# One operation per column for product and difference in a 32-step forward substitution

## The chip, the core and the metric

The kernel runs on one core of a Trainium2 chip. A core has a matrix engine (TensorE, PE in the rows; its weight loads are PEld), three engines for elementwise work (VectorE, DVE; ScalarE, ACT; GpSimd, POOL) and a queue that issues most transfers (SP). Each engine works through its own queue in order, and engines wait for each other by semaphores. The metric is the time of the program on the device in microseconds, median of the runs.

## What is computed

A decoder block on 256 tokens of width 2048: a SwiGLU block, a token mixer (8 gated DeltaNet heads beside 16 Mamba-2 heads), a second SwiGLU block and gated embeddings. The change is in the DeltaNet heads, in the inverse of a unit lower triangular matrix for each head and each chunk of tokens:

```python
lower = jnp.where(strict, jnp.einsum('bnhik,bnhjk->bnhij', kb, k) * decay, 0.0)
eye = jnp.eye(CHUNK, dtype=q.dtype)
t_inv = lax.linalg.triangular_solve(eye + lower, jnp.broadcast_to(eye, lower.shape),
                                    left_side=True, lower=True)
u = jnp.einsum('bnhij,bnhjv->bnhiv', t_inv, v * beta[..., None])
w = jnp.einsum('bnhij,bnhjk->bnhik', t_inv, kb * jnp.exp(gc)[..., None])
```

## The kernel before

All large products are float32 products made of pieces: a weight tile is loaded (`load`), each 128 x 1024 piece of it is rounded on ACT (`hi`, L118), the rest is taken on DVE (`lo`, L119), and PE multiplies both (`single`, L145 to L147: 8 blocks of three matmuls in a piece). There are four buffers each for `hi` and `lo`, so ACT and DVE can be four pieces ahead of PE and no more.

The mixer's input projection is 50 tiles of two such pieces, one after another, with the convolutions (L557), gates and scalings of each tile on DVE. The work of the heads is written as generators; `tick()` after each piece advances every open generator by one step, and the scheduler then puts the instructions of each engine in an order by dependences and a timeline of its own. So the work of the heads stands between pieces, in the queues of the same engines.

`gdn_pair(i, KQ, V)` does a pair of heads, and there are four pairs. A pair has four 128 x 128 matrices. It computes the lower triangles (`LA`, L601 to L609), writes their 32 x 32 diagonal blocks to memory (`blkl`, four transfers on POOL's queue, L630) and reads them back with the blocks spread over partitions (`Lb`, SP's queue, L632). Each of 128 partitions then holds one 32 x 32 block and four columns `Z[:, c, :]` of its inverse (`CG = 4`, `BS = 32`). `Z` starts as unit columns (L656). The substitution has 31 steps, three to a tick: step `j` multiplies the rest of column `j` of the block by `Z[:, c, j]` for all four columns at once into `tb` (L663), and takes it from the rest of `Z` (L665). A row `128x124` in the profile is four columns of 31, `128x4` four of 1. Then `Z` goes to memory (`blky`, L666), comes back in blocks (`Y`, four transfers, L671), is transposed (L674) and is merged in two levels by matmuls on PE (`ip`, `ix`, `iy`, L685) with masks and differences on DVE (L700, L690) between them; then follow the outputs of the two chunks (L714 to L758). `Lb`, `Z` and `tb` have one buffer each: the substitution of a pair begins when the one before has been stored.

Of the kernel before, what the change touches and what calls it, by code (L numbers as in the profile page):

```python
# [9 lines left out]
F32 = mybir.dt.float32  # L10
F32R = mybir.dt.float32r
AF = mybir.ActivationFunctionType
ALU = mybir.AluOpType
PSUM = bass.MemoryType.PSUM

P = 128
# [27 lines left out]
BS = 32  # L44
CG = 4
# [23 lines left out]
def tile_hybrid_block(ctx, tc, xT, pT, con, par, wgu1, wd1, wnar, win, wout, wgu2, wd2, wproj, wple, outT):  # L69
    nc = tc.nc  # L70
    act, dve, pool, pe = nc.scalar, nc.vector, nc.gpsimd, nc.tensor
# [25 lines left out]
    def over(ap, n):  # L97
        return ap.unsqueeze(1).to_broadcast([ap.shape[0], n, ap.shape[-1]])
# [263 lines left out]
    with ExitStack() as mix:  # L362
# [213 lines left out]
        def gdn_pair(i, KQ, V):  # L576
# [16 lines left out]
            for c in range(2):  # L593
# [5 lines left out]
                for hh in range(2):  # L599
                    m = 2 * c + hh  # L600
                    dve.scalar_tensor_tensor(out=LA[:, m, 0, :], in0=ps[:, hh * T:hh * T + P], scalar=1.0, in1=ident,  # L601
                                             op0=ALU.mult, op1=ALU.mult, accum_out=ss[:, m:m + 1])
# [4 lines left out]
                              in1=beta[:, :, h0:h0 + 2], op=ALU.mult)  # L607
            for m, (c, hh) in enumerate(mats):
                dve.scalar_tensor_tensor(  # L609
                    out=LA[:, m, :, :], in0=kk[c][:, hh * T:(hh + 1) * T].rearrange("p (a i) -> p a i", a=2),  # L610
                    scalar=c1[:, m:m + 1], in1=over(d[:, c, hh, :], 2), op0=ALU.mult, op1=ALU.mult)
# [19 lines left out]
            Lb = g2.tile([P, BS, BS], F32, tag="Lb", name="Lb", bufs=1)  # L631
            nc.sync.dma_start(Lb.rearrange("p j i -> p (j i)"),  # L632
                              bl.rearrange("q j i -> q (j i)").unsqueeze(1).to_broadcast([P // NG, NG, BS * BS]))
            Z = g2.tile([P, CG, BS], F32, tag="Z", name="Z", bufs=1)
            tb = g2.tile([P, CG * BS], F32, tag="tb", name="tb", bufs=1)

            Y = g2.tile([P, 4, P], F32, tag="Y", name="Y")
            pool.memset(Y, 0.0)
# [19 lines left out]
            for j in range(BS - 1):  # L658
                if j % STEP == 0:
                    yield  # L660
                n = BS - 1 - j
                t = tb[:, :CG * n].rearrange("p (c n) -> p c n", n=n)
                dve.tensor_tensor(out=t, in0=over(Lb[:, j, j + 1:], CG),  # L663
                                   in1=Z[:, :, j:j + 1].to_broadcast([P, CG, n]), op=ALU.mult)
                dve.tensor_tensor(out=Z[:, :, j + 1:], in0=Z[:, :, j + 1:], in1=t, op=ALU.subtract)  # L665
            nc.gpsimd.dma_start(by.rearrange("q c i -> (q c i)").rearrange("(p f) -> p f", p=P),  # L666
                              Z.rearrange("p c i -> p (c i)"))

# [62 lines left out]
            for hh in range(2):  # L731
                dve.scalar_tensor_tensor(out=y1[:, hh, :], in0=pk[:, hh, :], scalar=negc[:, h0 + hh:h0 + hh + 1],
                                         in1=y1[:, hh, :], op0=ALU.mult, op1=ALU.add)
# [28 lines left out]
        g2 = gdn_pool.enter_context(tc.tile_pool(name="g2", bufs=2))  # L762
# [4 lines left out]
        def delta_rule(i):  # L767
            KQ = g2.tile([P, 2, 2, T], F32, tag="KQ", name="KQ", bufs=3)
            V = g2.tile([P, 2, T], F32, tag="V", name="V", bufs=1)
            for which in range(3):  # L770
                j = 6 * i + 2 * which
                conv_silu(j, gcw[:, j:j + 2, :], None, V if which == 2 else KQ[:, :, which, :])
            drain([scalars_done])
            gdn.append(begin(gdn_pair(i, KQ, V)))
# [97 lines left out]
        for g in range(2):  # L872
            sacc = new_acc()
            for i in (2 * g, 2 * g + 1):
# [3 lines left out]
                                         op0=ALU.mult, op1=ALU.mult)  # L878
# [17 lines left out]
        op = mix.enter_context(tc.tile_pool(name="op", bufs=1))  # L896
# [48 lines left out]
    with tc.tile_pool(name="f2", bufs=2) as f2:  # L945
# [31 lines left out]
        for o in range(0, KD, 2):  # L977
            last = o == KD - 2
            t = f2.tile([P, 2, T], F32, tag="t", name="t")
            for j, n in ((0, 1), (1, 1)) if last else ((0, 2),):  # L980
# [4 lines left out]
                else:  # L985
                    for i in range(j, j + n):
# [5 lines left out]
                                         op0=ALU.add, op1=ALU.mult)  # L992
# [105 lines left out]
```

## Time and profile before

| | |
|---|---|
| median of 3 runs | 2078.45 us (2074.31 to 2078.91) |
| the profiled execution, own time | 2073.93 us |
| its span, first to last instruction | 2072.0 us |
| PE busy | 2049.0 us (99%) |
| DVE busy | 1362.2 us (66%) |
| ACT busy | 1035.1 us (50%) |
| POOL busy | 175.6 us (8%) |
| first product of the substitution to last difference | 838.0 to 1058.9 us |

Busy is the time in which an engine has at least one instruction under way. A span of 2072.0 us cut into 40 slices gives 51.8 us each, and the digits of the page are tenths of busy time in a slice. Times of rows are microseconds from the start of the span.

### The profile page before, as it was taken

The page shows a single profiled execution, that of the slowest core. Times are in us where ns is not written, and L with a number is a line of the kernel's source. Part 1 is how long each engine was busy: PE and PEld are TensorE (multiplying, and loading weights), DVE is VectorE, ACT ScalarE, POOL GpSimd, SP SyncE. Part 2 cuts the span into 40 slices and gives each one's busy share as a digit, 9 for nine tenths or more (in the row PEclk, how much of TensorE's full clock was granted, in tenths as well). Part 3 has the DMA queues.
Part 4 walks back from the last instruction along what each step waited for, and adds up shares of the span by engine and source line. Part 5 has one row for each costly group of instructions (what it writes and reads, how often), then busy time and mean ns, then how long its engine had stood idle before and what let it go on. Part 6 is the DMA issues. An engine that isn't in the chain of part 4 may idle for free.

```text
span 2072.0 us, 31523 instructions
## 1 busy us (share of the span) xinstructions
PE 2049.0 (99%) x12882; PEld 1832.2 (88%) x12882; DVE 1362.2 (66%) x2063; ACT 1035.1 (50%) x1544; POOL 175.6 (8%) x207
## 2 busy tenths in 40 slices
PE   9999999999999999999999999999999999999997
PEld 7888888888888889999999998888888888888886
DVE  7565555555656668999887666555555565556675
ACT  6444444444444555645545456444444444445554
POOL 2000000000000013413321111000000000000011
PEclk9999999999999999999999999999999999999998
DMA  7555555655555666554545555555556555545652
GB/s 266 190 186 183 171 176 194 211 183 183 186 184 178 197 219 218 184 179 164 162 166 173 190 179 189 190 183 184 167 184 217 182 184 185 191 162 190 208 183 102
DMA packets 64369, 384.58 MB, mean 186 GB/s; under 512 B 7616, under 2 KB 9168, under 8 KB 31072
## 3 DMA queue, kind: packets, MB, share of 16 engines
q1 hardware_dynamic: 61456, 376.75, 52.6%
q0 software_dynamic: 2480, 5.29, 0.8%
q8 instruction: 101, 1.65, 0.3%
q10 hardware_dynamic: 288, 0.52, 0.1%
q14 instruction: 44, 0.36, 0.0%
HBM read 377.78 MB, written 4.75 MB: 185 GB/s over the span
## 4 chain that ended last, share of the span: by engine, by line
PE 92%; DVE 3%; DMA 2%; issue 2%; POOL 1%; ACT 1%; POOLq 0%; DVEq 0%; SPq 0%; ACTq 0%
PE mm L130 50%; PE mm L128 24%; PE mm L146 4%; PE mm L147 4%; PE mm L145 4%; PE mm L132 1%; DVE lo L119 1%; DMA hT<-rows 1%; PE pj L130 0%; PE ip L685 0%; DMA blkl<-LA 0%; DMA blky<-Z 0%; DVE u L557 0%; PE iy L685 0%; POOL hT L820 0%
## 5 line engine op out<-in xcount | busy, mean ns | idle before, releaser
L119 DVE TENSOR_TENSOR lo<-raw,hi 128x1024 fp32r<-128x1024 f32 (+1 forms) x774 | 862.5, 1122 | 482.2 <-ACT hi L118 481.4
L130 PE MATMUL mm<-xs,hi 128*128 128x512 f32 x3088 | 1078.4, 397 | 0.7 <-DVE xs L190 0.7
L118 ACT CAST hi<-raw 128x1024 fp32r<-128x1024 f32 (+1 forms) x774 | 744.3, 963 | 558.8 <-PE mm L130 369.3
L128 PE MATMUL mm<-xs,lo 128*128 128x256 f32 x2895 | 812.7, 281 | 2.0 <-DVE lo L119 2.0
L130 PEld LDWEIGHTS mm<-xs,hi 128*128 128x128 f32 x3088 | 568.0, 188 | 124.6 <-DVE xs L190 1.2
L128 PEld LDWEIGHTS mm<-xs,lo 128*128 128x128 f32 x2895 | 543.5, 188 | 13.3 <-DVE lo L119 3.2
L130 PE MATMUL mm<-hid,hi 128*128 128x512 f32 x1408 | 492.5, 397 | 0.0
L128 PE MATMUL mm<-hid,lo 128*128 128x256 f32 x1344 | 377.8, 281 | 0.0
L130 PEld LDWEIGHTS mm<-hid,hi 128*128 128x128 f32 x1408 | 260.2, 188 | 59.0
L128 PEld LDWEIGHTS mm<-hid,lo 128*128 128x128 f32 x1344 | 253.3, 188 | 3.0
L147 PE MATMUL mm<-xs,lo 128*128 128x256 f32 x816 | 229.4, 281 | 3.4 <-DVE lo L119 3.4
L145 PE MATMUL mm<-xs,hi 128*128 128x256 f32 x816 | 229.7, 282 | 0.0
L146 PE MATMUL mm<-xs,hi 128*128 128x256 f32 x816 | 229.0, 281 | 0.0
L147 PEld LDWEIGHTS mm<-xs,lo 128*128 128x128 f32 x816 | 154.3, 189 | 4.1 <-DVE lo L119 4.0
L146 PEld LDWEIGHTS mm<-xs,hi 128*128 128x128 f32 x816 | 154.4, 189 | 0.4
L145 PEld LDWEIGHTS mm<-xs,hi 128*128 128x128 f32 x816 | 154.2, 189 | 0.6 <-issue 0.3
L168 ACT COPY t<-mm 128x256 f32<-128x256 f32 x167 | 62.2, 373 | 161.7 <-PE mm L130 160.6
L205 POOL TENSOR_TENSOR acc<-acc,sq 128x512 f32<-128x512 f32 x43 | 62.3, 1449 | 945.3 <-ACT sq L204 906.8
L169 DVE TENSOR_TENSOR t<-t,mm 128x256 f32<-128x256 f32 x167 | 69.9, 419 | 87.8 <-ACT t L168 87.5
L168 ACT COPY s<-mm 128x256 f32<-128x256 f32 x88 | 32.8, 372 | 149.0 <-PE mm L130 148.9
L169 DVE TENSOR_TENSOR s<-s,mm 128x256 f32<-128x256 f32 x88 | 37.1, 421 | 74.0 <-ACT s L168 73.9
L147 PE MATMUL mm<-osp,lo 128*128 128x256 f32 x256 | 71.8, 281 | 0.0
(304 smaller groups left out, 1444.1 us busy)
## 6 DMA issues: line engine op xcount, KB each, us to landing
raw<-in_wgu SPq DMA_DIRECT2D x173, 1024.0 KB, 4.8
raw<-in_wd SPq DMA_DIRECT2D x128, 704.0 KB, 4.1
raw<-in_win SPq DMA_DIRECT2D x52, 1024.0 KB, 4.8
raw<-in_wout SPq DMA_DIRECT2D x16, 1024.0 KB, 4.8
raw<-in_wple SPq DMA_DIRECT2D x16, 1024.0 KB, 4.8
first<-in_wgu SPq DMA_DIRECT2D x11, 256.0 KB, 7.2
hold<-hT POOLq DMA_DIRECT2D x4, 512.0 KB, 3.9
Lb<-blkl SPq DMA_DIRECT2D x4, 512.0 KB, 4.6
```

Of the source, the lines that this page charges most:

```text
L118: act.copy(hi, src)
L119: dve.tensor_tensor(out=lo, in0=src, in1=hi.bitcast(F32), op=ALU.subtract)
L128: pe.matmul(ps[:, 0, :], lo[:, w, :], act_in[:, k, 0, :], start=False, stop=False, skip_group_check=True)
L130: pe.matmul(ps, hi[:, w, :], act_in[:, k], start=start, stop=stop, skip_group_check=True)
L132: pe.matmul(ps[:, 0, :], lo[:, w, :], act_in[:, k, 0, :], start=False, stop=False, skip_group_check=True)
L145: pe.matmul(ps[:, 0, :], hi[:, i, :], act_in[:, k, 0, :], start=k == ks[0], stop=False)
L146: pe.matmul(ps[:, 0, :], hi[:, i, :], act_in[:, k, 1, :], start=False, stop=False)
L147: pe.matmul(ps[:, 0, :], lo[:, i, :], act_in[:, k, 0, :], start=False, stop=k == ks[-1])
L168: act.copy(out, ps[:, 0, :])
L169: dve.tensor_tensor(out=out, in0=out, in1=ps[:, 1, :], op=ALU.add)
L205: pool.tensor_tensor(out=acc, in0=acc, in1=sq, op=ALU.add)
```

## The change

The product and the difference of a step become one operation for each of the four columns, `Lb * z - Z` instead of `Z - Lb * z`. The sign of what remains turns at every step, so the odd entries of a column come out negated, and one multiplication by -1 on ACT turns them back before `Z` is stored. `tb` goes.

```diff
             Z = g2.tile([P, CG, BS], F32, tag="Z", name="Z", bufs=1)
-            tb = g2.tile([P, CG * BS], F32, tag="tb", name="tb", bufs=1)
...
             for j in range(BS - 1):
                 if j % STEP == 0:
                     yield
-                n = BS - 1 - j
-                t = tb[:, :CG * n].rearrange("p (c n) -> p c n", n=n)
-                dve.tensor_tensor(out=t, in0=over(Lb[:, j, j + 1:], CG),
-                                   in1=Z[:, :, j:j + 1].to_broadcast([P, CG, n]), op=ALU.mult)
-                dve.tensor_tensor(out=Z[:, :, j + 1:], in0=Z[:, :, j + 1:], in1=t, op=ALU.subtract)
+
+                for c in range(CG):
+                    dve.scalar_tensor_tensor(out=Z[:, c, j + 1:], in0=Lb[:, j, j + 1:], scalar=Z[:, c, j:j + 1],
+                                             in1=Z[:, c, j + 1:], op0=ALU.mult, op1=ALU.subtract)
+            odd = Z.rearrange("p c (i s) -> p c i s", s=2)[:, :, :, 1]
+            act.mul(odd, odd, -1.0)
             nc.gpsimd.dma_start(by.rearrange("q c i -> (q c i)").rearrange("(p f) -> p f", p=P),
                               Z.rearrange("p c i -> p (c i)"))
```

For a pair that is 124 operations in place of 62 on DVE, and one more on ACT. In the changed file the copy of unit columns is L655, the new operation L662, the negation L665 and the other lines named here up to one lower or the same.

The scheduler gives the engines another order. The first of three places is DVE's queue where the third pair begins. Before, two pieces `lo` of the projection stand between the last difference of the second pair (L665) and the copy that starts the third pair's `Z` (L656).

```order
L665 TENSOR_TENSOR Z<-Z,tb 128x4
L557 SCALAR_TENSOR_TENSOR u<-cin,gcw,u 128x256 x2
L119 TENSOR_TENSOR lo<-raw,hi 128x1024
L557 SCALAR_TENSOR_TENSOR u<-cin,gcw,u 128x256
L382 TENSOR_TENSOR cin<-mm,r 128x256
L119 TENSOR_TENSOR lo<-raw,hi 128x1024
L557 SCALAR_TENSOR_TENSOR u<-cin,gcw,u 128x256 x2
L656 COPY Z<-cont 128x128
```

The same place of the changed kernel, from the last step of the second pair (L662 `128x1`).

```order
L662 SCALAR_TENSOR_TENSOR Z<-Lb,Z 128x1 x4
L557 SCALAR_TENSOR_TENSOR u<-cin,gcw,u 128x256 x6
L382 TENSOR_TENSOR cin<-mm,r 128x256 x2
L655 COPY Z<-cont 128x128
L561 SCALAR_TENSOR_TENSOR V<-th,u 128x512
L662 SCALAR_TENSOR_TENSOR Z<-Lb,Z 128x31 x4
L662 SCALAR_TENSOR_TENSOR Z<-Lb,Z 128x30
L119 TENSOR_TENSOR lo<-raw,hi 128x1024
```

No piece stands between them any more. On ACT the negation of the second pair (L665) stands behind the scaling of the first pair's outputs (L753), which waits for a chain of small operations on POOL.

```order
L753 ACTIVATE o<-o,ro 128x128 x4
L552 ACTIVATE u<-cin,gcw 128x256 x2
L586 ACTIVATE ksq<-KQ 128x512
L665 ACTIVATE Z<-Z 128x64
```

The second place is DVE's queue where the fourth pair begins. Before: the last product and difference of the third pair (L663, L665 `128x4`) with a piece between them, two more pieces, the copy, a fourth piece.

```order
L663 TENSOR_TENSOR tb<-Lb,Z 128x4
L119 TENSOR_TENSOR lo<-raw,hi 128x1024
L557 SCALAR_TENSOR_TENSOR u<-cin,scw,u 128x256
L665 TENSOR_TENSOR Z<-Z,tb 128x4
L557 SCALAR_TENSOR_TENSOR u<-cin,scw,u 128x256
L814 TENSOR_TENSOR xd<-xt,sp 128x256 x2
L119 TENSOR_TENSOR lo<-raw,hi 128x1024
L557 SCALAR_TENSOR_TENSOR u<-cin,scw,u 128x256
L817 TENSOR_TENSOR xe<-xd,dte 128x256
L119 TENSOR_TENSOR lo<-raw,hi 128x1024
L656 COPY Z<-cont 128x128
L119 TENSOR_TENSOR lo<-raw,hi 128x1024
```

The same place of the changed kernel, from the last step of the third pair (L662 `128x1`) on, with the fourth pair's `LA` (L609) and the third pair's transpose (L674).

```order
L662 SCALAR_TENSOR_TENSOR Z<-Lb,Z 128x1
L609 SCALAR_TENSOR_TENSOR LA<-kk,c_9675,hT 128x256 x4
L614 TENSOR_TENSOR kdw<-c_9675,dte 128x2
L119 TENSOR_TENSOR lo<-raw,hi 128x1024
L814 TENSOR_TENSOR xd<-xt,sp 128x256 x2
L655 COPY Z<-cont 128x128
L817 TENSOR_TENSOR xe<-xd,dte 128x256
L662 SCALAR_TENSOR_TENSOR Z<-Lb,Z 128x31 x4
L662 SCALAR_TENSOR_TENSOR Z<-Lb,Z 128x30 x4
L674 STREAM_TRANSPOSE oT<-Y 128x512
L662 SCALAR_TENSOR_TENSOR Z<-Lb,Z 128x29 x4
```

One piece instead of two stands between the last step and the copy, `LA` of the fourth pair has moved to the place right behind that step, and the transpose stands behind the first eight new operations. No further `lo` follows until 69 of the fourth pair's 124 operations have been issued.

The third place is PE's queue at the merge of the third pair. Before, a piece of the projection (L145 to L147) stands between `iy` of the first level and `ip` of the second.

```order
L685 MATMUL iy_9843<-Y,blockQ 128x64 x4
L811 MATMUL xt<-cont,XS 128x128 x4
L145 MATMUL mm<-xs,hi 128x256
L146 MATMUL mm<-xs,hi 128x256
L147 MATMUL mm<-xs,lo 128x256
...
L685 MATMUL ip_9902<-oT,LA 128x64 x4
```

The same in the changed kernel.

```order
L758 MATMUL ot<-cont,o 128x128 x4
L685 MATMUL ip_9918<-oT,LA 128x64
L824 MATMUL ss_9924<-xe,Bt 128x256
L685 MATMUL ip_9918<-oT,LA 128x64 x3
L832 MATMUL py<-hT,xd 64x128 x8
L836 MATMUL yo<-BC,St 128x128 x2
L685 MATMUL ix_10023<-blockQ,Y 128x64 x4
L685 MATMUL iy_10028<-Y,blockQ 128x64 x4
L811 MATMUL xt<-cont,XS 128x128 x4
L685 MATMUL ip_10093<-oT,LA 128x64 x4
L145 MATMUL mm<-xs,hi 128x256
```

Here the first level, both differences and `ip` of the second level stand in one block without a piece of the projection between them. The merges of the second, third and fourth pair begin after 60, 74 and 86 of the 100 pieces before, and after 64, 76 and 87 now; the first after 44 before and 49 now.

## Rows read from the trace of the kernel before

**Rows 1.** Page, busy tenths in 40 slices.

```profile
PE   9999999999999999999999999999999999999997
DVE  7565555555656668999887666555555565556675
```

**Rows 2.** Busy time by stretch: PE, PEld, DVE, ACT, POOL, clock, DMA share, GB/s.

```profile
837.90:1058.90 221.00, 214.86 (x1853) 210.95 (x1852) 204.17 (x547) 117.33 (x215) 57.28 (x83) 0.99 0.51 176
880.00:900.00 20.00, 17.94 (x142) 17.73 (x142) 19.79 (x44) 8.46 (x12) 4.70 (x5) 0.91 0.46 163
1060.00:1160.00 100.00, 100.00 (x866) 99.71 (x865) 70.51 (x101) 52.79 (x84) 18.84 (x27) 1.00 0.50 173
```

**Rows 3.** Groups of DVE by line, 830 to 1062 us: busy, mean ns | idle before.

```profile
L665 DVE TENSOR_TENSOR Z<-Z,tb 128x124 f32<-128x124 f32 (+30 forms) x124 | 30.4, 245 | 1.3
L663 DVE TENSOR_TENSOR tb<-Lb,Z 128x124 f32<-128x124 f32 (+30 forms) x124 | 30.3, 245 | 4.9 <-DMA Lb<-blkl 3.5
```

**Rows 4.** DVE in order of time: start, duration in us, instruction [idle before].

```profile
935.23 0.21 DVE L663 TENSOR_TENSOR tb<-Lb,Z 128x48 f32<-128x48 f32 x1
935.47 0.21 DVE L665 TENSOR_TENSOR Z<-Z,tb 128x48 f32<-128x48 f32 x1
...
936.45 0.34 DVE L732 SCALAR_TENSOR_TENSOR xv<-ks,negc,xv 128x128 f32<-128x128 f32 x1
936.71 0.68 DVE L561 SCALAR_TENSOR_TENSOR KQ<-th,u 128x512 f32<-128x512 f32 x1
...
939.00 0.48 DVE L557 SCALAR_TENSOR_TENSOR u<-cin,gcw,u 128x256 f32<-128x256 f32 x1
939.39 0.19 DVE L663 TENSOR_TENSOR tb<-Lb,Z 128x36 f32<-128x36 f32 x1
939.51 0.48 DVE L557 SCALAR_TENSOR_TENSOR u<-cin,gcw,u 128x256 f32<-128x256 f32 x1
```

**Rows 5.** Waits of DVE, then of PE, 837.9 to 1058.9: total us, times, longest.

```profile
DVE Z L656 <- DMA blky<-Z: 5.1, 3, 3.0
DVE tb L663 <- DMA Lb<-blkl: 3.5, 1, 3.5
DVE lo L119 <- ACT hi L118: 2.3, 3, 1.1
...
PE ip L685 <- DVE oT L674: 3.0, 2, 1.6
PE mm L147 <- DVE lo L119: 2.3, 2, 2.1
```

**Rows 6.** DVE in order of time where the fourth pair begins.

```profile
1000.89 1.26 DVE L609 SCALAR_TENSOR_TENSOR LA<-kk,c,hT 128x256 f32<-128x256 f32 x3
...
1003.74 0.16 DVE L665 TENSOR_TENSOR Z<-Z,tb 128x4 f32<-128x4 f32 x1
...
1012.02 0.23 DVE L656 COPY Z<-cont 128x128 f32<-128x128 f32 x1 [3.05 <-DMA blky<-Z]
...
1016.87 0.29 DVE L663 TENSOR_TENSOR tb<-Lb,Z 128x124 f32<-128x124 f32 x1 [3.49 <-DMA Lb<-blkl]
...
1020.01 0.71 DVE L674 STREAM_TRANSPOSE oT<-Y 128x512 f32<-128x512 f32 x1
```

**Rows 7.** POOL in order of time at the same place.

```profile
1006.54 0.59 POOL L666 DMA_DIRECT2D blky<-Z  x1
...
1012.28 2.21 POOL L671 DMA_DIRECT2D Y<-blky  x4 [1.83 <-DMA blky<-Z]
```

**Rows 8.** PE in order of time, within one piece.

```profile
1014.73 0.28 PE L145 MATMUL mm<-xs,hi 128*128 128x256 f32 x1
...
1016.43 0.28 PE L145 MATMUL mm<-xs,hi 128*128 128x256 f32 x1
```

**Rows 9.** DVE in order of time after the last difference of the fourth pair.

```profile
1058.77 0.16 DVE L665 TENSOR_TENSOR Z<-Z,tb 128x4 f32<-128x4 f32 x1
...
1067.28 0.70 DVE L674 STREAM_TRANSPOSE oT<-Y 128x512 f32<-128x512 f32 x1
```

## The prediction

> **What bounds the kernel now.** I read the page first. PE is busy in every slice, and DVE, at 66% over the span, reaches nine tenths in slices 17 to 19, which lie in the mixer [rows 1]. The table by stretch says more: from the first product of the substitution to the last difference, 221.0 us, DVE is busy for 204.2 and PE for 214.9; from 1060 to 1160 us DVE needs 70.5 of 100 and PE all of it [rows 2]. So PE sets the time of the whole, but in the stretch that the change touches DVE has 221.0 - 204.2 = 16.8 us left and little else to give. The waits say how PE stays fed: it waits for `lo` for 2.3 us in the stretch, and for the transpose before a merge for 3.0 [rows 5]. Of DVE's own 16.8 us, 5.1 are waits of the copy that starts `Z` for the store of the pair before, and 3.5 a wait for `Lb` [rows 5]: the chain of the pairs, not spare time.
>
> **The price of one new operation.** DVE starts an instruction that waits for nothing before the one ahead has ended, so I count from start to start. An operation of this kind with a scalar per partition takes 936.71 - 936.45 = 0.26 us for 128 columns and 939.39 - 939.00 = 0.39 for 256 [rows 4], that is 1.02 ns a column and 0.13 us fixed. The new ones have 31 to 1 columns, 16 on average: 0.13 + 0.016 = 0.146 us. There are 4 pairs x 31 x 4 = 496: 72.4 us. No row shows one so small. A bound from below is the small product, 939.51 - 939.39 = 0.12 us for 36 columns [rows 4], 0.10 for 16; a bound from above is the duration at 128 columns less 112 columns, 0.34 - 0.114 = 0.226 us, which it would take if each waited for the one ahead. It need not: it reads what the operation four places before it wrote, and 4 x 0.146 = 0.58 us is longer than 0.226. I take 0.146 because its kind and scalar are those of the two rows it comes from.
>
> [...]
>
> **What they replace.** The 248 old ones, L663 and L665, last 30.3 + 30.4 = 60.7 us [rows 3]. A product overlaps its neighbour by 0.07 us where that does not wait (0.19 long, next start after 0.12), and where the difference follows directly, the gap is 0.24 for 0.21 [rows 4]. Added from start to start, without idle time, they take 48.3. So DVE gets 72.4 - 48.3 = +24 us; with 0.13 to 0.16 us for one, +16 to +31.
>
> **What covers it.** Of the 16.8 us that DVE idles, 8.6 belong to the chain of the pairs; the rest is waits for `hi` and the like, which vanish when DVE is late. I take 6 (4 to 8). Then PE has pieces in store: four buffers, and a piece is 24 matmuls of (1016.43 - 1014.73) / 15 = 0.113 us [rows 8], 2.7 us. Of 4 x 2.7 = 10.9 I take half, 5 us (3 to 8), which is used up once.
>
> **What the new order adds.** Where the third pair begins, six operations of 0.39 us on `u` and two on `cin` of about 0.3 stand between the last step and the copy, 3 us, and the copy must wait for the store. In the row of before the store took from 1006.54 to 1012.02, 5.5 us [rows 6, 7]: at least 2.5 us idle. The negation comes first, and on ACT it stands behind scalings that wait for POOL. At most I give it 9, and I take 7; before, a copy waited 3.0 at most and the three together 5.1 [rows 5].
>
> Where the fourth pair begins, `Lb` sets the pace. From the end of L609 (1000.89 + 1.26 = 1002.1) to the first product, 14.8 us pass [rows 6], for two transfers one after the other. Before, DVE had work there and idled 3.05 + 3.49 = 6.5 us. Now L609 stands behind the last step, and there are only L614, one `lo` (1.1), two L814, the copy and L817 for it, 2.3 us: idle 12.5, so +6 (0 to 9). The transpose of the third pair stands behind the first eight new operations and waits with them. PE meanwhile stands before `ip` with no piece of the projection ahead of the whole first level, and 69 new operations follow on DVE before the next `lo`. That is how DVE's delay reaches PE.
>
> At the end, the fourth pair's transpose came 1067.28 - 1058.77 = 8.5 us after the last difference [rows 9], and PE did not wait. Now the negation lies between, and PE is no longer pieces behind DVE. Store and reload took 1020.01 - 1006.54 = 13.5 us at the third pair [rows 6, 7]; PE has two pieces and some small work for it, 6 to 7 us: +6 (0 to 9).
>
> Last, the clock. Between 880 and 900 us, with 2.06 us of PE idle, the granted clock was 0.91 of full speed [rows 2], 1.8 us lost at most. Two such losses: +3 (0 to 6).
>
> The negation itself, four small operations on ACT, which has 104 of 221 us free [rows 2], costs only what it adds to the store, counted above.
>
> **Sum.** +24 - 6 + 7 + 6 = +31 for DVE at the last step; -5 for PE's store of pieces; +6 and +3: **+35 us**. The profiled execution took 2073.93 us, so 2109. It is the fast end of the runs (median 2078.45); I add half the distance, **2111 us**. All small ends at once give +16 - 8 - 8 = 0, all large ones +31 - 4 + 9 + 9 - 3 + 9 + 6 = +57, 2133. The small ones exclude each other in part, since pieces in store are used up only where DVE is late; I let this case begin at +13, 2089.
>
> **Rivals.**
> *Work alone.* The stalls at the pairs stay what they were, because the chains have as much cover as before. Then +24 - 6 - 5 = +13, and 1 for the clock: 2090. For it: the transfers were waited for 8.6 us in all. Against: the order has taken the pieces away that stood there.
> *Small operations are cheap.* At 0.10 us, 496 take 50 us against 48.3, so DVE is as loaded as before, and only the order remains: +7 + 6 - 6 - 5 = +2 to +10 with the last pair's wait: 2078 to 2086. For it: the row of 0.12 for 36 columns. Against: each row with a scalar per partition lies about 0.06 above a product of its width. [...]
> *Faster.* Products and differences that wait for each other go: 0.24 us for 0.12 [rows 4]. If the new operation costs under 0.08 us, 496 take 40 us, DVE gains 8, and PE can win back the 3.0 + 2.3 us of its waits [rows 5], at most 5: 2071. It decides at 0.08 us, and with that the stalls must stay away too. Against: the fixed 0.13 us, and the block of 69 operations before a `lo`.
> *Each waits for the one ahead.* At 0.226 us they take 112 us, +64: +64 - 6 + 7 + 6 - 5 + 9 = +75, 2151. Against: other columns lie between.
>
> **Chances.** The forecast 0.62, work alone 0.18, cheap 0.10, faster 0.04, serial 0.06. The forecast and work alone make 0.80 and reach from 2086 (work alone with 4 us less) to 2136 (the large ends with a level 3 us higher, as the median has it), which is the range. About 0.2%, 4 us, is what a measurement of this kernel can tell from no change. Slower by more: 0.62 + 0.18 + 0.06 and half of the cheap case, 0.92; within: 0.05; faster: 0.03.
>
> **What would show it.** In the profile of the changed kernel: L662 with 496 rows at about 0.15 us from start to start and 0.22 to 0.25 long; DVE busy over 97% between the pairs; waits of L655 for the store and of L662 for `Lb` of 12 to 25 us together; PE idle by 20 us or more in one place before `ip` of the third pair and again before that of the fourth, with a lower clock behind it; nothing changed before 838 us and after the mixer. I am wrong if PE's waits for `lo` and the transpose stay under 10 us in all, or if one new operation takes 0.10 us or less. If DVE is full as said and PE waits less than 20 us, then I have the pieces in store too small.

## The result and the profile after

The changed kernel takes 2106.44 us (median of 4 runs, 2105.21 to 2107.08), the kernel before 2077.47 on the same chip: a ratio of 1.014, 95% interval 1.0127 to 1.0152. It is 29 us slower; the forecast was 2111. The profiled execution took 2107.08 us with a span of 2105.0, 33.0 more than before.

First the group of the new operation (line, shapes, count, busy, mean ns, idle before), 836 to 1110 us, where [rows 3] has the two old ones, and its price in DVE's queue (start, duration), where [rows 4] stood.

```profile
L662 DVE SCALAR_TENSOR_TENSOR Z<-Lb,Z 128x31 f32<-128x31 f32 (+30 forms) x496 | 96.0, 243 | 5.0 <-DMA Lb<-blkl 5.0
```

```profile
1016.50 1.81 DVE L662 SCALAR_TENSOR_TENSOR Z<-Lb,Z 128x17 f32<-128x17 f32 x12
1018.24 1.21 DVE L119 TENSOR_TENSOR lo<-raw,hi 128x1024 fp32r<-128x1024 f32 x1
```

Twelve operations of 17 to 14 columns in 1018.24 - 1016.50 = 1.74 us are 0.145 us each. One lasts 0.22 us (median; the mean of 0.243 has some long ones in it), so each overlaps the one behind it by about 0.08.

Next the busy time by stretch (columns as in [rows 2]).

```profile
837.90:1058.90 221.00, 193.30 (x1627) 189.31 (x1625) 204.54 (x677) 104.44 (x194) 48.69 (x79) 0.95 0.48 162
840.00:880.00 40.00, 39.12 (x335) 38.71 (x334) 40.00 (x131) 23.56 (x42) 9.02 (x13) 1.00 0.56 189
980.00:1020.00 40.00, 39.10 (x346) 38.25 (x345) 40.00 (x121) 21.08 (x34) 3.82 (x5) 1.00 0.41 147
1020.00:1040.00 20.00, 13.15 (x99) 11.88 (x97) 15.61 (x76) 7.49 (x21) 10.29 (x20) 0.89 0.53 157
1040.00:1060.00 20.00, 8.29 (x58) 7.69 (x58) 12.00 (x56) 2.55 (x9) 5.07 (x8) 0.60 0.30 90
```

Within a pair DVE (third number behind the length) has no gap at all. Yet over the 221.0 us it idles 16.5, as much as before (16.8): what it no longer idles elsewhere it idles between 1020 and 1060, where PE does 21.4 us of work in 40 and the granted clock falls to 0.60.

The waits say for what: DVE's from 836 to 1110, then PE's from 836 to 1165 (total, times, longest), beside [rows 5].

```profile
DVE Z L655 <- DMA blky<-Z: 9.1, 3, 7.4
DVE Z L662 <- DMA Lb<-blkl: 5.0, 1, 5.0
```

```profile
PE ip L685 <- DVE oT L674: 15.6, 4, 12.4
PE mm L147 <- DVE lo L119: 5.2, 3, 2.2
PE ot L758 <- ACT o L753: 5.0, 2, 4.3
PE mm L145 <- DVE cin L382: 4.0, 1, 4.0
PE xt L811 <- DVE LA L609: 1.8, 1, 1.8
PE mm L145 <- DVE zt L382: 1.8, 1, 1.8
```

PE waits 33.4 us in all in place of 6.1 in the same stretch before. That is 27.3 of the 33.0. Here is the place, DVE's queue and then PE's in order of time (idle before in brackets); [rows 6] has DVE's before.

```profile
1034.87 0.74 DVE L814 TENSOR_TENSOR xd<-xt,sp 128x256 f32<-128x256 f32 x2
1043.05 0.23 DVE L655 COPY Z<-cont 128x128 f32<-128x128 f32 x1 [7.44 <-DMA blky<-Z]
1043.19 0.42 DVE L817 TENSOR_TENSOR xe<-xd,dte 128x256 f32<-128x256 f32 x1
1048.56 2.37 DVE L662 SCALAR_TENSOR_TENSOR Z<-Lb,Z 128x31 f32<-128x31 f32 x8 [4.95 <-DMA Lb<-blkl]
1050.86 0.70 DVE L674 STREAM_TRANSPOSE oT<-Y 128x512 f32<-128x512 f32 x1
```

```profile
1032.97 0.66 PE L811 MATMUL xt<-cont,XS 128*128 128x128 f32 x4 [1.83 <-DVE LA L609]
1037.88 1.35 PE L758 MATMUL ot<-cont,o 128*128 128x128 f32 x4 [4.25 <-ACT o L753]
1051.61 0.69 PE L685 MATMUL ip<-oT,LA 128*128 128x64 f32 x2 [12.38 <-DVE oT L674]
```

DVE waits for the store and then for `Lb`; the third pair's transpose stands behind that and the first eight new operations; PE stands before the third pair's `ip` and has no piece of the projection ahead of it. In the trace `Lb` landed at 1048.47 and the last part of the third pair's `Y` at 1048.84, so the eight operations hold the transpose back by 2 us and no more; negation, store and reload set the rest. From the third pair's last step to its transpose 18.9 us pass (1031.9 to 1050.9), and 16.3 before (1003.7 to 1020.0): the transpose comes 30.8 us later, and 28.2 of that is DVE's lateness at the last step.

How late each was, by the start of the last operation of each pair's substitution, and by the start of the first matmul of a piece of the projection (counted from 0):

| | before | after | later by |
|---|---|---|---|
| DVE, last step of pair 1 | 897.7 | 911.5 | 13.8 |
| pair 2 | 951.7 | 972.3 | 20.6 |
| pair 3 | 1003.7 | 1031.9 | 28.2 |
| pair 4 | 1058.8 | 1093.2 | 34.4 |
| PE, piece 74 | 1017.5 | 1021.7 | 4.3 |
| piece 76 | 1030.9 | 1061.7 | 30.8 |
| piece 84 | 1063.6 | 1094.4 | 30.8 |
| piece 98 | 1112.2 | 1145.1 | 32.9 |

DVE falls behind by 6 to 14 us with every pair. From the first operation of the substitution to the last, DVE takes 253.4 us in place of 220.8: 31.8 more for the substitution itself, 1.7 less for other work, 2.6 more idle time (counted as in the experiments below). PE shows little of it up to piece 74, since its order puts the merges behind more pieces (64 instead of 60 at the second pair). Then it pays nearly everything between pieces 75 and 76.

Most of the rest of the 33 us is the clock. Three stretches of after (columns as in [rows 2]):

```profile
971.00:973.00 2.00, 2.00 (x11) 2.00 (x10) 1.49 (x8) 0.06 (x1) 1.51 (x7) 0.50 0.72 291
1044.00:1051.00 7.00, 0.00 (x0) 0.00 (x0) 2.44 (x9) 1.28 (x4) 4.32 (x7) 0.50 0.34 84
1053.00:1055.00 2.00, 2.00 (x13) 1.83 (x13) 2.00 (x13) 0.37 (x1) 0.00 (x0) 0.50 0.00 0
```

The granted clock was at half speed (0.50) for 3.4 us from 970.6, for 20.5 from 1035.4 and for 3.4 from 1062.7; before only once in this part of the span, for 3.4. From 1062.7 to 1066.1 a matmul of a piece started every 0.213 us, and at full clock every 0.113. PE worked in some 12 of these 27 us, so it lost about 6 by my estimate, against 2 before: +4 to 5.

### The profile page after: what moved, and what is told of

It reads as the page before. It is cut to its first block, busy times and chain, and to the rows that moved or that the text cites. A ratio compares the mean times of both kernels' runs of the same rounds, so it can differ in the third digit from the quotient of the medians.

```text
span 2105.0 us, 31810 instructions
## 1 busy us (share of the span) xinstructions
PE 2054.3 (98%) x12882; PEld 1835.9 (87%) x12882; DVE 1395.4 (66%) x2311; ACT 1033.9 (49%) x1548; POOL 174.4 (8%) x207
## 4 chain that ended last, share of the span: by engine, by line
PE 85%; DVE 7%; DMA 3%; issue 2%; POOL 1%; ACT 1%; SPq 0%; POOLq 0%; DVEq 0%; ACTq 0%
PE mm L130 49%; PE mm L128 24%; PE mm L145 3%; PE mm L146 3%; PE mm L147 3%; DVE Z L662 2%; DVE lo L119 2%; PE mm L132 1%; DVE u L557 1%; DMA hT<-rows 1%; DMA blky<-Z 1%; DMA hT<-in_xT 0%; PE pj L130 0%; DMA blkl<-LA 0%; POOL hT L820 0%
## 5 line engine op out<-in xcount | busy, mean ns | idle before, releaser
L128 PEld LDWEIGHTS mm<-xs,lo 128*128 128x128 f32 x2895 | 543.5, 188 | 13.8 <-DVE lo L119 3.7
L145 PE MATMUL mm<-xs,hi 128*128 128x256 f32 x816 | 230.7, 283 | 5.8 <-DVE cin L382 4.0
L147 PE MATMUL mm<-xs,lo 128*128 128x256 f32 x816 | 230.1, 282 | 5.2 <-DVE lo L119 5.2
L145 PEld LDWEIGHTS mm<-xs,hi 128*128 128x128 f32 x816 | 155.0, 190 | 6.5 <-DVE cin L382 4.2
L147 PEld LDWEIGHTS mm<-xs,lo 128*128 128x128 f32 x816 | 154.8, 190 | 6.1 <-DVE lo L119 5.8
L168 ACT COPY s<-mm 128x256 f32<-128x256 f32 x88 | 32.8, 373 | 149.2 <-PE mm L130 149.1
L662 DVE SCALAR_TENSOR_TENSOR Z<-Lb,Z 128x31 f32<-128x31 f32 (+30 forms) x496 | 96.0, 243 | 5.0 <-DMA Lb<-blkl 5.0
```

Of the source, the lines that this page charges most:

```text
L128: pe.matmul(ps[:, 0, :], lo[:, w, :], act_in[:, k, 0, :], start=False, stop=False, skip_group_check=True)
L145: pe.matmul(ps[:, 0, :], hi[:, i, :], act_in[:, k, 0, :], start=k == ks[0], stop=False)
L147: pe.matmul(ps[:, 0, :], lo[:, i, :], act_in[:, k, 0, :], start=False, stop=k == ks[-1])
L168: act.copy(out, ps[:, 0, :])
L662: dve.scalar_tensor_tensor(out=Z[:, c, j + 1:], in0=Lb[:, j, j + 1:], scalar=Z[:, c, j:j + 1], in1=Z[:, c, j + 1:], op0=ALU.mult, op1=ALU. ...
```

## The experiments

The time of the kernel before is 2076.4 to 2077.5 beside each. The substitution's share of DVE is counted alike for all: from the start of each of its operations to the start of the next instruction on DVE, idle gaps of more than 0.1 us left out. By that count the kernel before has 51.1 us and the changed one 82.9. The 48.3 of the prediction leave out the short gaps too, of 0.03 us mostly, behind old operations that wait for the one ahead; the new ones have none.

The scheduler makes a new order for each of these kernels, so an edit changes the places of the work too, and where that bears on a result it is said.

**A constant for the scalar.** Price, or number of operations and their order?

```diff
-    scalar=Z[:, c, j:j + 1],
+    scalar=0.5,
```

> The 496 new operations stay, with their shapes and their order in a step, but the factor is the constant 0.5 instead of a scalar per partition, so the substitution itself is left out and the output is not that of the block; all else stays. My theory: the price of an operation with a scalar per partition is what fills DVE. An operation with a constant should start every 0.08 to 0.11 us, 40 to 55 us for 496 in place of 83, about what the old form took (48); then the third pair's merge comes while pieces of the projection still stand ahead of it on PE, and the time is 2075 to 2088. Rival: the number of operations, whatever one costs: 2100 or more.

2082.75 us, ratio 1.0032 (1.0019 to 1.0046). One place of DVE's queue, with 16 columns:

```profile
858.15 0.44 DVE L662 SCALAR_TENSOR_TENSOR Z<-Lb,Z 128x16 f32<-128x16 f32 x4
858.49 0.30 DVE L601 SCALAR_TENSOR_TENSOR LA<-kk,cont 128x128 f32<-128x128 f32 x1
```

0.34 us for four, 0.085 each; all 496 take 51.7. The same operation in the same number costs what the old form did, and 23 of the 29 us are gone. The scalar per partition adds 0.06 us to an operation (0.145 less 0.085), and this is the price that the change pays. The order is another one too, with the merges after 40, 54, 68 and 80 pieces. Six microseconds stay; the second last group of experiments comes back to them.

**Without the negation.**

```diff
-            odd = Z.rearrange("p c (i s) -> p c i s", s=2)[:, :, :, 1]
-            act.mul(odd, odd, -1.0)
```

> The negation on ACT is left out, so every second entry of the inverse's columns has the wrong sign; all else is the changed kernel. My theory: the negation adds only to the store of Z, and the long idle of PE ahead of the third pair's merge comes from DVE's load: within 4 us of the changed kernel, 2102 to 2108. Rival: the chain over ACT (scalings that wait for POOL, then the negation, then the store) is what makes the pairs late: 2095 or less.

2104.22 us, ratio 1.0136 (1.0121 to 1.0152), within the noise of the changed kernel. The copy's waits for the store fell from 9.1 to 0.5, and the wait for `Lb` rose from 5.0 to 12.2: the same gap under another name.

**The same operation on ACT in the kernel before.**

```diff
+            odd = Z.rearrange("p c (i s) -> p c i s", s=2)[:, :, :, 1]
+            act.mul(odd, odd, 1.0)
```

> The kernel before, with an operation on ACT over the odd entries of Z (a scaling by 1) before the store, where the changed kernel negates. The substitution stays as it was. My theory: 0 to +3, 2076 to 2080, as the store of Z is not the last to arrive at the pairs before. Rival: the longer store is a wait of its own, the +7 and +6 that I gave to the starts of the pairs and the fourth's end: 2083 or more.

2076.38 us, ratio 0.9998 (0.9988 to 1.0007). The negation costs nothing that can be told from noise on either side.

**The new form in half of the pairs.** The old form stands in the other two (`if i < 2` and `if i > 1`).

> The new form in the first two pairs alone, the old one in the last two; DVE gets about 17 us more, all before the third pair. Rival, simple addition: half of the loss, 2090 to 2094. My theory after the traces: the loss arises in one place, ahead of the third pair's merge on PE, where the order has no piece of the projection left (piece 76), and every delay of DVE until then that pushes the merge to that place costs PE the rest of the chain: here the order puts the merge at piece 76 too, so 2096 to 2108, and PE idles 8 us or more in one place before it.

> The new form in the last two pairs alone. DVE gets about 17 us more, half of it before the third pair's merge. Simple addition: 2090 to 2094. My theory: the order puts the third pair's merge at piece 76 here too, so 2094 to 2106, though DVE is less late there than with the new form in the first two pairs; both together lose more than the changed kernel does.

First two pairs: 2092.29 us, 1.0084 (1.0067 to 1.0101). Last two: 2091.17 us, 1.0073 (1.0058 to 1.0088). The halves cost 15.9 and 14.8 us, together 30.7 against 29 to 30 for the whole: plain addition. My theory of that moment, that being late at piece 76 costs most of the loss however late one is, falls. Its place was right: PE was 6.4 and 2.9 us late at piece 74, and 17.5 and 16.2 at piece 76. PE's longest waits with the new form in the first two pairs, and then in the last two:

```profile
PE ip L693 <- DVE oT L682: 5.5, 1, 5.5
PE mm L145 <- DVE cin L382: 4.1, 1, 4.1
```

```profile
PE ip L693 <- DVE Z L663: 11.4, 1, 11.4
```

So piece 76 is where PE pays, and DVE's lateness is what it pays.

**Load on DVE that has nothing to do with the chain.**

```diff
                 dve.tensor_tensor(out=Z[:, :, j + 1:], in0=Z[:, :, j + 1:], in1=t, op=ALU.subtract)
+                for k in range(2):
+                    dve.tensor_tensor(out=wk[:, 2 * k], in0=wk[:, 2 * k + 1], in1=wk[:, 2 * k + 1], op=ALU.mult)
```

> The kernel before, with two more products of 128x36 on DVE behind each of the 124 steps, on a tile that nothing else reads: 248 operations of about 0.12 us, some 30 us of DVE. Neither the substitution's own operations nor the transfers are changed. Theory after the first four runs: what costs is DVE's time in the stretch between the first copy and the last step, whatever it is spent on, less the 6 to 10 us that DVE idled there: +20 to +28, 2096 to 2105. Rival: the new operations cost by the chain that they form (a step's result is the next one's scalar), so unchained operations fill DVE's idle time: under 2090.

2111.68 us, ratio 1.0165 (1.015 to 1.018), above my range. The 248 products took 32.8 us (each gap counted up to 0.4), the substitution 2.7 more than before: +35.5 on DVE and +34.2 in the time. All of them (count, shortest, median and longest in ns, first and last start), those behind 836 us, and PE's largest wait of that kernel:

```profile
L669 DVE TENSOR_TENSOR wk<-wk x248: 130/188/1511, 763.0 to 944.2; 128x36 f32<-128x36 f32 x124
L669 DVE TENSOR_TENSOR wk<-wk 128x36 f32<-128x36 f32 x124 | 29.3, 278 | 0.0
```

```profile
PE ip L689 <- DVE oT L678: 11.1, 2, 6.7
```

Work that nobody waits for costs as much here as the new operations do, so the chain that they form is not needed for a loss of this size. But the products did not stay behind their steps. The order put 167 of them ahead of the first product of the substitution, which came at 861.0 instead of 838.0, and the rest among the first pair's steps. The first pair's last step came 55 us later than before, the fourth's 25. PE lost its time at other places too, and its clock was at half speed for 30.7 us in the mixer; it worked in 24.6 of them. So this run shows what load on DVE can cost, and not that the same load in the places of the new operations costs the same.

**Another spread of the same work.** Two steps to a tick in the changed kernel; the third pair's merge then stands at piece 80.

```diff
-STEP = 3
+STEP = 2
```

> The changed kernel with two steps of the substitution to a tick instead of three; nothing else. DVE's work is the same, but the order puts the third pair's merge at piece 80 of the projection instead of 76, with two pieces of lo between the fourth pair's copy and the third pair's transpose. If DVE's load sets the time: 2098 to 2112, with the idle time of PE spread over more places or moved to the fourth pair. Rival: the block without pieces before the third pair's merge is itself the cost: 2094 or less.

2102.1 us, ratio 1.012 (1.0105 to 1.0135). The place that cost 27 us is gone, as the stretches and DVE's waits show; the last row is one of PE's waits:

```profile
1020.00:1040.00 20.00, 18.35 (x164) 17.81 (x163) 19.59 (x68) 11.50 (x30) 6.73 (x10) 1.00 0.59 206
1040.00:1060.00 20.00, 18.65 (x141) 17.59 (x142) 19.59 (x45) 11.26 (x22) 12.29 (x17) 0.91 0.46 142
```

```profile
DVE Z L655 <- DMA blky<-Z: 4.6, 3, 3.7
PE ot L758 <- ACT o L753: 6.3, 2, 5.4
```

No wait for `Lb` is left, DVE idles 9.8 us from 836 to 1110 instead of 23.7, and still 4 us are all that comes back. PE's waits are in other places now (6.4 for `cin`, 6.3 for the outputs on ACT, 3.0 for `zt`). The edit moves the fourth pair as well: its merge begins after 96 pieces instead of 87, and its outputs stand behind the last piece with nothing of the projection beside them. Against the kernel before, PE is 12.9 us late at piece 99 and 26.1 at the first product behind the projection. So half of the loss arises at the end in this order, and the 4 us are what the whole order gives back; what the block before the third merge was worth by itself is not shown.

**Two buffers for `Z`.**

```diff
-            Z = g2.tile([P, CG, BS], F32, tag="Z", name="Z", bufs=1)
+            Z = g2.tile([P, CG, BS], F32, tag="Z", name="Z", bufs=2)
```

> The changed kernel with two buffers for Z instead of one, so the copy of a pair's unit columns no longer waits for the store of the pair before (9.1 us of DVE's idle time in the changed kernel); nothing else is taken out. If that wait is part of the loss: 2096 to 2102. If Lb, which follows two transfers later, sets the start of a pair anyway, the wait moves to the first operation of the new pair: 2103 to 2108. My theory is the second.

2107.85 us, ratio 1.0147 (1.0132 to 1.0162). DVE's and PE's longest waits:

```profile
DVE Z L662 <- DMA Lb<-blkl: 14.8, 3, 12.9
```

```profile
PE ot L758 <- ACT o L753: 14.3, 1, 14.3
```

The 9.1 us of the copy went to `Lb`, whose two transfers begin with `LA` and not with the store. In the changed kernel `Lb` and the reload of `Y` landed within 0.4 us of each other, so with one of the two waits gone the other is left. In the kernel before, the same edit:

> The kernel before with two buffers for Z. The copy's waits for the store (5.1 us of DVE) go, and its order puts the copy of each pair earlier. With two buffers the changed kernel did not gain, since Lb comes later still: here -2 to +3, 2075 to 2080. If the waits of the pairs' chain carried the time: 2072 or less.

2079.95 us, ratio 1.0014 (1.0005 to 1.0024). Nothing is gained there either. Two buffers for `Lb`, 4 kB more in each partition, were not tried.

**What order alone does.** The constant again, and the kernel before, both with `STEP = 2`.

> The constant 0.5 in place of the scalar per partition (the substitution itself left out), with two steps to a tick instead of three. With a constant the 496 operations took 51.7 us against the old form's 51.1, yet the time was 6 us above before. If that rest is the order alone, another order at the same load moves it: within 5 us of before, 2073 to 2082, or again several us off, but not by the same PE wait of 3.1 us before a merge at piece 40. If the rest comes from the number of operations, it stays at 2081 to 2085.

> The kernel before with two steps to a tick instead of three. In the changed kernel this took the block before the third pair's merge away and gave 4 us back. Here there is no such block, PE waits for 7 us in all in the stretch: -3 to +4, 2074 to 2081. If the spread of a pair over more pieces is worth 4 us at any load: 2074 or less.

2081.74 us, 1.0022 (1.0012 to 1.0032), and 2077.94, 1.0004 (0.9995 to 1.0013). With the constant 4.3 of the 6.4 us stay in the other order. The two intervals overlap, so no gain is shown, and 2081.74 lies in both of my ranges: this pair of runs does not decide between the order and the number of operations. The wait for the merge fell from 3.1 to 1.8. The substitution's load is 49.6 us there, under that of before, and its last step comes at 1046.3, 12 us earlier. So neither load nor lateness explains what stays. In the first constant kernel the clock does for the most part; three stretches of it:

```profile
836.40:839.50 3.10, 3.10 (x16) 3.10 (x16) 3.06 (x10) 3.10 (x10) 0.69 (x2) 0.50 0.70 200
901.20:907.80 6.60, 4.37 (x20) 4.37 (x21) 6.60 (x28) 2.59 (x5) 0.00 (x0) 0.50 0.43 159
1013.90:1020.50 6.60, 6.60 (x31) 6.60 (x32) 6.08 (x28) 1.74 (x3) 0.00 (x0) 0.50 0.45 160
```

PE was at half speed for 17.1 us there and worked in 14.6 of them, so it lost 7.3 us by my estimate (half of that), against 1.7 before, while its waits grew only from 6.1 to 7.4. With two steps to a tick it was at half speed for 6.8 us and worked in all of them; there most of the 4.3 stays open.

**Less load on DVE.** The products on POOL, the differences still on DVE.

```diff
-                dve.tensor_tensor(out=t, in0=over(Lb[:, j, j + 1:], CG),
+                pool.tensor_tensor(out=t, in0=over(Lb[:, j, j + 1:], CG),
```

> The kernel before with the 124 products of the substitution on POOL instead of DVE; the differences stay on DVE. DVE's load falls by the products' 25 us, so if DVE's load alone set the time, PE's waits of 7 us in the stretch would go: 2070 to 2074. Rival: the step now crosses between the engines twice, POOL takes about 3 ns a column (1.53 us for 512) and lies under the transfers that it issues, so a pair lasts longer and the merges come late: 2085 to 2110. I hold the rival the likelier, six to four.

2081.56 us, ratio 1.0021 (1.0011 to 1.0031), under the range of my rival and above that of the load. From 837 to 1060 us DVE is busy for 187.5 instead of 205.3. POOL's group and DVE's wait for it:

```profile
L663 POOL TENSOR_TENSOR tb<-Lb,Z 128x124 f32<-128x124 f32 (+30 forms) x124 | 66.4, 535 | 66.2 <-DVE Z L665 61.1 <-DMA Lb<-blkl 4.2 <-DVE ss L603 0.7
```

```profile
DVE Z L665 <- POOL tb L663: 13.9, 40, 1.7
```

17.8 us less on DVE bring nothing: PE had waited for only 6.1 us in all, and DVE now waits for POOL. In these runs more load on DVE costs 0.7 to 1.0 us a microsecond, and the one run with less gains nothing. None of these kernels is faster than the one before by more than the noise.

| kernel | substitution and extra work on DVE, against before | time, against before |
|---|---|---|
| changed | +31.8 | +29.0 |
| without negation | +32.5 | +27.8 |
| two steps to a tick | +34.5 | +24.7 |
| new form in pairs 1, 2 | +19.2 | +15.9 |
| new form in pairs 3, 4 | +14.7 | +14.8 |
| extra products | +35.5 | +34.2 |
| constant | +0.6 | +6.4 |

## Why the forecast held, step by step

- **The price, 0.146 us: right.** 0.145 in the row above, 0.161 at 31 columns and 0.130 at one (medians). The rival of cheap operations fell with it: at 16 columns 0.085 from start to start is what a constant scalar showed, and a scalar per partition 0.145. The 0.06 that the prediction gives a scalar per partition above a product of its width is in the trace of before at 256 columns, from start to start: two products L814 take 940.71 - 940.04 = 0.67 us, 0.335 each, and L557 takes 0.39.
- **The work, +24: too small by 10.5.** By the prediction's count, without any gaps, it is 82.9 - 48.3 = +34.6; by the table's it is +31.8. I took 48.3 us for the old operations from a sum that held their hold-ups beside POOL, and 72.4 for the new ones from a price without any. Eleven of the 496 last 0.54 to 1.34 us, each beside an operation on POOL, and add 10.3 us, which is the whole of the error; before there were seven, some 6 us.
- **The cover, -6: right.** By the same count, outside the waits of the pairs' chain DVE's idle time fell from 8.2 us (16.8 - 8.6) to 2.4 (16.5 - 14.1). The chain's own waits grew by 5.5, so that the sum stayed; the next two terms are these waits.
- **The third pair's start, +7: wrong, about 0.** From the second pair's last step to the third pair's first operation 7.8 us passed before and 7.3 after; the copy waited 1.1 in place of 0.2. The runs with and without the negation show that the chain I feared has cover.
- **The fourth pair's start, +6: right.** DVE idled 7.44 + 4.95 = 12.4 us there in place of 6.5, +5.9, and 12.5 was the forecast. For the last step of all I forecast +31; it came 34.4 later, since the missing 10.5 of the work stood against the 7 of the third pair's start.
- **PE's store of pieces, -5: about -8, and the picture does not hold.** PE is 30.8 us late at piece 84, with 4 to 5 of the clock in it, where DVE's last step is 34.4 late. With the third pair's last step 28 us late PE was 4.3 late at piece 74: more cover than the 10.9 us that four buffers hold, because the order puts the merges behind more pieces. At piece 76 it was used up at once.
- **The fourth pair's transpose, +6: too large.** PE waited 1.2 us there; its delay grew from 30.8 us at piece 84 to 32.9 at piece 98.
- **The clock, +3: 4 to 5** by the estimate above. The lower clock lay in the wait and behind it.

Of what I named as signs, the price, DVE full within the pairs and 14.1 us of waits of L655 and L662 came; PE's idle time before the third pair's `ip` came to 18.5 us in three parts, a little under the 20 named, and there was none like it before the fourth pair's. PE's waits for `lo` and the transpose were 20.8, over the 10 below which I was to be wrong. "Work alone" had the cause right, but not its size, nor the fourth pair's start; with +34.6 for the work its sum gives 2101. That the forecast lay only 5 us off (2 by the profiled executions, +35 against +33.0) is partly luck, as an error of -10.5 in the work stood against +7, +4 and +3 in the third pair's start, the last transpose and the store.

## What to carry to other kernels

Before merging two operations over all columns into one for each column, count start to start: four small operations of 0.145 us against two of about 0.2 is a loss, however many operands it saves. An engine that is 66% busy over the span can be full in the one stretch that matters; there each further microsecond of work cost 0.7 to 1.0 us of time here, even where the waits named other things, and a wait that was taken away came back under another name as long as the load stayed. Where a scheduler makes the order, look in the trace where the work of an experiment came to stand before reading its time. Count old and new by the same rule, with the hold-ups in both or in neither.

## What the runs showed of the hardware

- The same DVE operation with a scalar per partition starts every 0.145 us at 16 columns and with a constant every 0.085.
- Eleven of the 496 new operations last 0.54 to 1.34 us in the changed kernel, where the median is 0.22, each beside an elementwise operation of 256 or 512 columns on POOL. Here DVE's queue and POOL's at 886 us:

```profile
885.91 2.52 DVE L662 SCALAR_TENSOR_TENSOR Z<-Lb,Z 128x10 f32<-128x10 f32 x2
888.35 1.58 DVE L557 SCALAR_TENSOR_TENSOR u<-cin,gcw,u 128x256 f32<-128x256 f32 x1
```

```profile
885.74 6.56 POOL L820 TENSOR_TENSOR hT<-hT,CB 128x512 f32<-128x512 f32 x5 [5.62 <-DVE CB L793]
```

  Two operations of ten columns take 2.44 us instead of 0.28 while POOL runs products of 512 columns. With the constant the longest of the 496 still takes 1.31 us.
- After PE's wait of 4.0 us at 967 to 971 us the granted clock was at half speed for 3.4 us, and for 20.5 us around the waits of 4.3 and 12.4 us before the third pair's merge it was there again.
